# A recurrent layer rearranged: x blocks first, y blocks last, float32 gates, gelu in one function, warm-up matmuls

## The chip, the cores and the metric

The kernel runs on one core of one Trainium2 chip. The metric is the device time of one execution in microseconds (us). Three runs of the kernel before took 1265.87, 1268.60 and 1271.18 us, so their median is 1268.6.

## What is computed

The program is a decoder of two layers over 512 positions of width 1024, all in float32. The first layer is recurrent, the second is attention, and each is followed by a SwiGLU feed-forward. The change is in the recurrent layer:

```python
def recurrent_mixer(h, w_in, conv_w, conv_b, ga_w, ga_b, gx_w, gx_b, lam, w_out):
    proj = h @ w_in                                    # h: rms-normed, 512 x 1024; proj: 512 x 2048
    y_branch, x_branch = jnp.split(proj, 2, axis=-1)
    gate = jax.nn.gelu(y_branch, approximate=True)
    xc = causal_depthwise_conv(x_branch, conv_w, conv_b)          # 4 taps
    hr = rg_lru(xc, ga_w, ga_b, gx_w, gx_b, lam)
    return (gate * hr) @ w_out

# rg_lru, with block-diagonal gates of 8 blocks of 128 x 128:
    r_gate = sigmoid(einsum(xb, w_a) + b_a);  i_gate = sigmoid(einsum(xb, w_x) + b_x)
    log_a = -8 * r_gate * softplus(-lam);     a = exp(log_a)
    u = sqrt(-expm1(2 * log_a)) * (i_gate * x)
    h[t] = a[t] * h[t-1] + u[t]
```

## The kernel before, in words

Activations lie transposed: eight tiles of 128 channels x 512 positions. A float32 value is held as two float32r halves, high and low, and a product is three float32r matmuls (`mm3`: high by high, low by high, high by low, lines 134 to 136). A weight block of 128 output channels (128 x 1024 elements, 512 KB) comes by `Stream`: it is loaded into a ring of two buffers `wr` on SP's DMA queue (line 78), ScalarE casts the high half (line 92), and the low half is made either by a subtract on VectorE (line 99) or, for eight of the sixteen input blocks, by a negating pass on ScalarE (line 95) and a DMA of GpSimd that adds the weights from memory (line 96). Three pairs of halves are held at a time. These casts and subtracts are given a high priority.

A scheduler takes the instructions in program order, with the priorities, and lays down at compile time the order in which every engine issues them; each engine then runs its list in that order and waits where an operand isn't there yet. There are eight PSUM banks: four tagged "mm" for the block products, two "PT", one "S" and one "O".

The recurrent layer (lines 259 to 427) runs so. x comes as eight tiles, and each is scaled by the norm's gain and split (line 205 on ScalarE, 206 on VectorE). The first two input blocks run side by side over k as the tiles come. Then the squares of x are summed (`squares`), the third block runs, and after it come the norm's factors: column sums by TensorE (line 226), some ten small VectorE steps (`rsqrt`), a product of a float32 128 x 512 tile with ones (line 239) and a copy by ScalarE to `rb` (line 241). No result of an input block leaves its PSUM bank before `rb` is there, since `x_block` and `y_block` multiply by it first (lines 332 and 395).

The sixteen input blocks follow `lru_order`: x blocks are numbers 8 to 15, y blocks 0 to 7, and from the sixth on x and y blocks take turns. `x_block` writes the scaled rows, does the convolution (ScalarE one tap, VectorE three) and splits the result. Two blocks later `x_gates` does the two gate products, each by `mm3`, then two sigmoids, a tanh and a product. After each four x blocks `recur` does the decay by exp, a Square, the square root, and the scan in time on VectorE (line 386). `act_order` keeps runs of one activation function together on ScalarE, since a change of function set costs an `ACT_TABLE_LOAD`. `y_block` does the gelu in four steps around a Square and a tanh; `y_gate` multiplies by the scanned state and splits. The gate weights are loaded through the same ring `wr`, on ScalarE's DMA queue, and split (`load_gates`). The output product then takes eight blocks one after the other, each over all eight gated blocks in the order of k.

## Time and profile before

| | |
|---|---|
| time of the profiled execution | 1268.64 us |
| its span | 1266.9 us |
| TensorE matmul, busy | 1218.9 us (96%), 5634 instructions |
| VectorE, busy | 705.9 us (56%) |
| ScalarE, busy | 521.2 us (41%) |
| GpSimd, busy | 192.6 us (15%) |
| mean granted clock of TensorE | 0.984 |

The span runs from the first instruction to the last; a clock of 1.00 is the full level of 2.4 GHz, 0.5 the low one of 1.2 GHz. A TensorE instruction's recorded length overlaps that of the next, so the distance between two starts is its cost. In the rows, PE is TensorE, DVE VectorE, ACT ScalarE, SP the DMA queue of that name, and L134 is line 134.

### The profile page before, as it was taken

The numbers are of one execution on the slowest core, as the hardware profiler recorded it, in microseconds if no ns is written. First come the engines' busy times: TensorE is split into PE (matmuls) and PEld (weight loads), VectorE is DVE, ScalarE is ACT, GpSimd is POOL, SyncE is SP. The second block draws the span as 40 slices with busy tenths as digits, with TensorE's granted clock in tenths as the row PEclk, the third lists the DMA queues.
The fourth block names the chain that finished last, engine by engine and source line by source line (L and its number), as shares of the span: only waits on it lengthen the run. The fifth ranks groups of instructions, "written<-read, shape, count | busy, mean of one in ns | idle before, by whom it ended". The sixth has DMA issues, their size and how long they took to land.

```text
span 1266.9 us, 14906 instructions
## 1 busy us (share of the span) xinstructions
PE 1218.9 (96%) x5634; PEld 1010.3 (80%) x5634; DVE 705.9 (56%) x1292; ACT 521.2 (41%) x964; POOL 192.6 (15%) x172
## 2 busy tenths in 40 slices
PE   7899899999999999999998899899999999999998
PEld 6678688888888888887876777888888888888887
DVE  7788855554455333396566665785754455552221
ACT  5798532332322222266534554554432322332210
POOL 0100001111011000011333355422111011110000
PEclk9899999999999999999999999799999999999999
DMA  5454232223332333332422121001323332223431
GB/s 200 123 135 114 78 100 87 96 100 100 100 100 92 95 93 107 105 102 84 132 68 82 52 67 51 17 18 51 99 85 101 100 100 96 89 94 100 122 119 46
DMA packets 36649, 117.19 MB, mean 93 GB/s; under 512 B 4449, under 2 KB 6625, under 8 KB 36577
## 3 DMA queue, kind: packets, MB, share of 16 engines
q1 hardware_dynamic: 34416, 110.17, 27.6%
q0 software_dynamic: 1152, 4.19, 1.8%
q10 hardware_dynamic: 1008, 1.88, 0.5%
q8 instruction: 44, 0.72, 0.2%
q14 instruction: 29, 0.23, 0.1%
HBM read 113.08 MB, written 2.10 MB: 91 GB/s over the span
## 4 chain that ended last, share of the span: by engine, by line
PE 78%; DVE 12%; ACT 7%; issue 1%; DMA 1%; SPq 0%; DVEq 0%; ACTq 0%
PE ps L135 22%; PE ps L134 22%; PE ps L136 22%; DVE kn L600 3%; PE ps L641 3%; PE ps L643 3%; PE ps L642 3%; ACT junk L583 1%; ACT wh L92 1%; PE ps L716 1%; PE ps L786 1%; DVE kn L610 1%; DVE wl L99 1%; DVE pr L771 1%; DVE gated L386 1%
## 5 line engine op out<-in xcount | busy, mean ns | idle before, releaser
L92 ACT CAST wh<-wr 128x1024 fp32r<-128x1024 f32 (+2 forms) x206 | 210.9, 1024 | 506.8 <-PE ps L135 443.2
L134 PE MATMUL ps<-xh,wh 128*128 128x512 f32 x896 | 353.5, 395 | 12.1 <-ACT xh L205 6.0
L136 PE MATMUL ps<-xh,wl 128*128 128x512 f32 x896 | 351.1, 392 | 0.0
L135 PE MATMUL ps<-xl,wh 128*128 128x512 f32 x896 | 350.8, 391 | 0.0
L99 DVE TENSOR_TENSOR wl<-wr,wh 128x1024 fp32r<-128x1024 f32 (+2 forms) x166 | 240.0, 1447 | 151.9 <-ACT wh L92 151.8
L134 PEld LDWEIGHTS ps<-xh,wh 128*128 128x128 f32 x896 | 169.4, 189 | 48.2 <-DVE xp L332 6.3
L136 PEld LDWEIGHTS ps<-xh,wl 128*128 128x128 f32 x896 | 169.3, 189 | 35.6 <-issue 0.2
L135 PEld LDWEIGHTS ps<-xl,wh 128*128 128x128 f32 x896 | 169.5, 189 | 35.3 <-issue 0.5
L136 PE MATMUL ps<-gh,wl 128*128 128x512 f32 x352 | 137.1, 389 | 0.0
L134 PE MATMUL ps<-gh,wh 128*128 128x512 f32 x352 | 137.1, 389 | 0.0
L135 PE MATMUL ps<-gl,wh 128*128 128x512 f32 x352 | 137.1, 389 | 0.0
L451 POOL TENSOR_TENSOR u<-u,g 128x512 f32<-128x512 f32 x44 | 58.7, 1334 | 507.3 <-ACT wh L92 363.8
L450 DVE TENSOR_TENSOR u<-ps,rb 128x512 f32<-128x512 f32 x44 | 30.4, 691 | 139.2 <-PE ps L136 139.2
L99 POOL TENSOR_TENSOR wl<-wr,wh 128x1024 fp32r<-128x1024 f32 x32 | 77.1, 2409 | 193.2 <-ACT wh L92 141.8
L641 PE MATMUL ps<-wh,xh 128*128 128x512 f32 x224 | 93.2, 416 | 0.0
L643 PE MATMUL ps<-wh,xl 128*128 128x512 f32 x224 | 89.4, 399 | 0.0
L642 PE MATMUL ps<-wl,xh 128*128 128x512 f32 x224 | 89.1, 398 | 0.0
L134 PEld LDWEIGHTS ps<-gh,wh 128*128 128x128 f32 x352 | 66.1, 188 | 13.8
L136 PEld LDWEIGHTS ps<-gh,wl 128*128 128x128 f32 x352 | 66.1, 188 | 13.6
L135 PEld LDWEIGHTS ps<-gl,wh 128*128 128x128 f32 x352 | 66.1, 188 | 13.6
L448 DVE TENSOR_TENSOR g<-ps,rb 128x512 f32<-128x512 f32 x44 | 30.4, 691 | 63.9 <-PE ps L136 63.8
L209 ACT CAST gh<-u 128x512 fp32r<-128x512 f32 x44 | 27.4, 622 | 60.8 <-POOL u L451 60.8
(213 smaller groups left out, 1558.7 us busy)
## 6 DMA issues: line engine op xcount, KB each, us to landing
wr<-in_f_in SPq DMA_DIRECT2D x88, 512.0 KB, 3.5
wr<-in_f_out SPq DMA_DIRECT2D x32, 512.0 KB, 3.5
wr<-in_w_q SPq DMA_DIRECT2D x24, 512.0 KB, 3.5
wr<-in_w_in SPq DMA_DIRECT2D x14, 512.0 KB, 4.1
wr<-in_f_out SPq DMA_DIRECT2D x16, 384.0 KB, 3.1
wr<-in_w_kv SPq DMA_DIRECT2D x12, 512.0 KB, 3.5
wl<-in_w_in POOLq DMA_DIRECT2D x8, 512.0 KB, 7.2
wr<-in_a_out SPq DMA_DIRECT2D x8, 512.0 KB, 3.7
```

The costliest lines, as they stand in the source:

```text
L92: nc.scalar.copy(hi[:, c], r[:, c])
L99: eng.tensor_tensor(lo[:, c], r[:, c], hi[:, c].bitcast(F32), ALU.subtract)
L134: PE.matmul(ps, wh, xh, start=first, stop=False)
L135: PE.matmul(ps, wh, xl, start=False, stop=False)
L136: PE.matmul(ps, wl, xh, start=False, stop=last)
L448: V.tensor_tensor(g, pair[0], rb, ALU.mult)
L450: V.tensor_tensor(u, pair[1], rb, ALU.mult)
L451: G.tensor_tensor(u, u, g, ALU.mult)
L600: V.scalar_tensor_tensor(dst[:, c], dst[:, c], r[:, nh * t + i:nh * t + i + 1], grow[:, g_row, :], ALU.mult, ALU.mult)
L641: PE.matmul(ps[t], xh[k][:, r], wh[:, c], start=k == 0, stop=False)
L642: PE.matmul(ps[t], xh[k][:, r], wl[:, c], start=False, stop=False)
L643: PE.matmul(ps[t], xl[k][:, r], wh[:, c], start=False, stop=k == 7)
```

## The change

The diff does these things. A float32 product of ones runs ten times ahead of everything else on TensorE. The parameters and the first weight block are loaded on ScalarE's DMA queue instead of SP's. The splits of x are held in their order and given a high priority, as are the squares, and the next VectorE subtract of a weight block is put behind the last sum of squares. The norm's column sums stand in the middle of the third block and its row factors in the middle of the fourth; the factors are copied by VectorE; a fifth block uses a bank tagged "PT" before the factors are needed. All x blocks come before all y blocks. The gate weights stay float32, in buffers of their own on SP's queue, and each gate product is one float32 product in place of three float32r matmuls. The root of the decay is taken from a tanh of half the argument and multiplied by 1 + a, with no Square. The gelu is one activation function, after the last square root. The y blocks are gated when both halves of the recurrence are done. The first two output blocks run side by side over k.

The diff, cut to its core:

```diff
@@ -47,6 +47,12 @@
     return a, b, v - a - b
 
 
+def behind(tc, inst, f):
+
+    tc.add_manual_dep(inst.ins, f.ins.name, mybir.DependencyInfo(
+        mybir.DependencyClass.NoSync, mybir.DependencyReason.DATA), reason="order")
+
+
 class Pool:
 
 
...
+
+    def _load(self, i, queue=None):
         ap = self.pieces[i][0]
         r = self.pool.tile([128, 1024], F32, name=f"wr{i}", tag="wr", bufs=2)
         w = ap.shape[-1]
         self.raw[i] = (r, w)
-        return [lambda c=c: self.nc.sync.dma_start(r[:, c], ap[:, c]) for c in self._cuts(i, w)]
+        return [lambda c=c: (queue or self.nc.sync).dma_start(r[:, c], ap[:, c]) for c in self._cuts(i, w)]
 
     def _cuts(self, i, w):
         return [slice(0, 512), slice(512, 1024)] if i < self.halved else [slice(0, w)]
...
+                    a = eng.tensor_tensor(lo[:, c], r[:, c], hi[:, c].bitcast(F32), ALU.subtract)
+                    if self.hold and eng is nc.vector:
+                        behind(self.tc, a, self.hold)
+                        self.hold = None
 
         return [lambda c=c: do(c) for c in self._cuts(i, w)]
...
-    def start(self, n):
...
 
         self.halved = self.nl = self.ns = n
-        loads, splits = zip(*[(self._load(i), self._split(i)) for i in range(n)])
+        loads, splits = zip(*[(self._load(i, None if i else first), self._split(i)) for i in range(n)])
         return [[x[j] for x in y] for y in (loads, splits) for j in range(2)]
 
     def load_to(self, i):
...
 
-    lru_order = [8, 9, 10, 11, 12, 0, 13, 1, 14, 2, 15, 3, 4, 5, 6, 7]
+    lru_order = [8, 9, 10, 11, 12, 13, 14, 15, 0, 1, 2, 3, 4, 5, 6, 7]
     p_in = add_pieces([A["w_in"][m] for m in lru_order[:4]])
...
                 step()
 
-        load_a, load_b, split_a, split_b = ws.start(2)
-        nc.sync.dma_start(par, A["par"])
+        G.memset(ones, 1.0)
+        load_a, load_b, split_a, split_b = ws.start(2, nc.scalar)
+        nc.scalar.dma_start(par, A["par"])
         for k in range(KB):
             nc.sync.dma_start(h[k], A["x"][k])
             run(load_a if k == 0 else load_b if k == 2 else ())
-        G.memset(ones, 1.0)
+        idle = bank("S")
+        for _ in range(10):
+            PE.matmul(idle[:, 0:128], ones, ones, start=True, stop=True)
         G.memset(ident, 0.0)
         G.affine_select(ident, ident, pattern=[[-1, 128]], compare_op=ALU.not_equal, fill=1.0,
                         base=0, channel_multiplier=1)
...
 
         def split(src, gain, hi, lo):
-            S.activation(hi, src, AF.Copy, scale=gain)
+            a = S.activation(hi, src, AF.Copy, scale=gain)
             V.scalar_tensor_tensor(lo, src, gain, hi.bitcast(F32), ALU.mult, ALU.subtract)
+            return a
 
         def halve(src, hi, lo, eng=None):
...
-                V.tensor_add(ssum, ssum, sq)
+                return V.tensor_add(ssum, ssum, sq)
 
         def gain(c, k):
...
 
-        def norm_rows(pool, r, tag="sq", bufs=1):
+        def norm_rows(pool, r, tag="sq", bufs=1, copy=S.copy):
...
             rb = pool.tile([128, T], F32, name="rb", bufs=1)
-            S.copy(rb, ps)
+            copy(rb, ps)
             return rb
 
         def out_proj(p0, nk, per, act_h, act_l, after):
...
             small = Pool(ls)
             for k in range(KB):
-                split(h[k], gain(C_AN, k), xh[k], xl[k])
+                with tc.high_priority():
+                    a = split(h[k], gain(C_AN, k), xh[k], xl[k])
+                    if k:
+                        behind(tc, a, before)
+                    before = a
                 run(split_a if k == 0 else split_b if k == 3 else ())
-            def in_block(i):
-                ps = bank()
+
+            def in_block(i, tag="mm", between=None):
+                ps = bank(tag)
                 wh, wl = ws.get(i)
                 for k in range(KB):
                     c = slice(128 * k, 128 * k + 128)
                     mm3(ps, (wh[:, c], wl[:, c]), (xh[k], xl[k]), k == 0, k == KB - 1)
+                    if k == 3 and between:
+                        between()
                 return ps
 
             parts = [ws.get(0), ws.get(1)]
...
                 for ps, (wh, wl) in zip(first, parts):
                     mm3(ps, (wh[:, c], wl[:, c]), (xh[k], xl[k]), k == 0, k == KB - 1)
-            for k in range(KB):
-                squares(k, lp, "q", 2)
-            first.append(in_block(2))
-            r = norm_factors(small)
-            rb = norm_rows(lp, r, "q", 2)
+            gw = [lp.tile([128, 1024], F32, name=f"gw{i}", bufs=1) for i in range(2)]
+            for g in range(2):
+                nc.sync.dma_start(gw[g], A["gates"][g])
+            with tc.high_priority():
+                for k in range(KB):
+                    ws.hold = squares(k, lp, "q", 4)
+            norm = []
+
+            def soon(fn, *args):
+                with tc.high_priority():
+                    norm.append(fn(*args))
+
+            first.append(in_block(2, between=lambda: soon(norm_factors, small)))
+            first.append(in_block(3, between=lambda: soon(norm_rows, lp, norm[0], "q", 4, V.tensor_copy)))
+            rb = norm[1]
+            first.append(in_block(4, "PT"))
 
 
             lam = par[:, C_LAM:C_LAM + 8]
-            sp8, nsp8 = (small.tile([128, 8], F32, name=n, bufs=1) for n in ("sp8", "nsp8"))
+            sp4, nsp8 = (small.tile([128, 8], F32, name=n, bufs=1) for n in ("sp4", "nsp8"))
             l1 = small.tile([128, 8], F32, name="l1", bufs=1)
             l2 = small.tile([128, 8], F32, name="l2", bufs=1)
...
+            V.tensor_scalar(sp4, sp4, 4.0, None, ALU.mult)
 
             def perm(t):
                 return t.rearrange("q (n i p) -> q n p i", n=4, i=32, p=4)
...
+            hgh = [lp.tile([128, T], F32R, name=f"hgh{k}", bufs=1) for k in range(KB)]
+            hgl = [lp.tile([128, T], F32R, name=f"hgl{k}", bufs=1) for k in range(KB)]
+
+            gated = [lp.tile([128, T], F32, name=f"gated{k}", bufs=1) for k in range(KB)]
+            rate, tau, runs, done = [None] * 4, [None] * 4, [], []
 
             def act_order(inst):
 
-                tc.add_manual_dep(inst.ins, last_act[0].ins.name, mybir.DependencyInfo(
...
             def x_block(b, i):
                 ps = first.pop(0) if first else in_block(i)
-                xp = lp.tile([128, 640], F32, name="xp")[:, :T + 4]
+                xp = lp.tile([128, 640], F32, name="xp", bufs=3)[:, :T + 4]
                 G.memset(xp[:, 0:3], 0.0)
                 V.tensor_tensor(perm(xp[:, 3:3 + T]), mine(ps), mine(rb), ALU.mult)
-                xc = lp.tile([128, T], F32, name="xc", bufs=3)
...
-
-            def x_gates(b, xc, ch, cl):
+                return b, xc
+
...
-                mm3(pr, (gw[0][:, c], gw[1][:, c]), (ch, cl), True, True)
-                mm3(pi, (gw[2][:, c], gw[3][:, c]), (ch, cl), True, True)
+                PE.matmul(pr, gw[0][:, c], xc, start=True, stop=True)
+                PE.matmul(pi, gw[1][:, c], xc, start=True, stop=True)
                 sl = slice(T * (b % 2), T * (b % 2) + T)
                 if b % 2 == 0:
                     rate[b // 2] = lp.tile([128, 2 * T], F32, name="rate", bufs=3)
                     tau[b // 2] = lp.tile([128, 2 * T], F32, name="tau", bufs=3)
                 r = rate[b // 2][:, sl]
-                if b % 4 == 0 and b:
-                    act_order(S.activation(r, pr, AF.Sigmoid, bias=gain(C_GA, b)))
-                else:
-                    S.activation(r, pr, AF.Sigmoid, bias=gain(C_GA, b))
...
             def recur(half):
 
-
+                end_run()
                 for j in range(4):
                     b = 4 * half + j
-                    sl = slice(T * (b % 2), T * (b % 2) + T)
-                    a, t = rate[b // 2][:, sl], tau[b // 2][:, sl]
-                    e = S.activation(a, a, AF.Exp, scale=nsp8[:, b:b + 1])
-                    if j == 0:
-                        act_order(e)
-                    q = lp.tile([128, T], F32, name="q")
...
+                    V.scalar_tensor_tensor(gated[b], a, 1.0, gated[b], ALU.add, ALU.mult)
+                end_run()
                 for j in range(2):
                     t = tau[2 * half + j]
-                    e = S.activation(t, t, AF.Sqrt, scale=0.25)
-                    if j == 0:
-                        act_order(e)
+                    done.append(S.activation(t, t, AF.Sqrt))
+                    act_order(done[-1])
                     for i in range(2):
                         b = 4 * half + 2 * j + i
                         sl = slice(T * i, T * i + T)
                         V.tensor_tensor(gated[b], gated[b], t[:, sl], ALU.mult)
                         V.tensor_tensor_scan(gated[b], rate[b // 2][:, sl], gated[b], 0.0, ALU.mult, ALU.add)
-                last_act[0] = e
-
-            hgh = [lp.tile([128, T], F32R, name=f"hgh{k}", bufs=1) for k in range(KB)]
-            hgl = [lp.tile([128, T], F32R, name=f"hgl{k}", bufs=1) for k in range(KB)]
+                end_run()
 
             def y_block(b, i):
-                ps = first.pop(0) if first else in_block(i)
-                y = lp.tile([128, T], F32, name="y")
+                ps = in_block(i)
+                y = lp.tile([128, T], F32, name="y", bufs=4)
                 V.tensor_tensor(y, ps, rb, ALU.mult)
-                t = lp.tile([128, T], F32, name="t", bufs=3)
-                S.activation(t, y, AF.Square, scale=math.sqrt(0.044715))
-                V.scalar_tensor_tensor(t, t, 1.0, y, ALU.add, ALU.mult)
-                S.activation(t, t, AF.Tanh, scale=math.sqrt(2.0 / math.pi))
-                V.scalar_tensor_tensor(t, t, 1.0, y, ALU.add, ALU.mult)
-                return b, t
-
-            def y_gate(b, t):
-                V.tensor_tensor(mine(t), mine(t), perm(gated[b]), ALU.mult)
-                halve(t, hgh[b], hgl[b])
-
-            load_gates()
+                return b, y
+
+            def y_gate(b, y):
+                g = S.activation(y, y, AF.Gelu_apprx_tanh)
+                act_order(g)
+                V.tensor_tensor(mine(y), mine(y), perm(gated[b]), ALU.mult)
+                halve(y, hgh[b], hgl[b])
+
             xs, ys, halves = [], [], 0
             for i, m in enumerate(lru_order):
                 if m < 8:
...
                         recur(halves)
                         halves += 1
-                while ys and ys[0][0] < 4 * halves:
+                while ys and halves == 2:
                     y_gate(*ys.pop(0))
 
-            def after_a(m):
+            def end_a(m, ps):
+                V.tensor_add(h[m], h[m], ps)
                 split(h[m], gain(C_AF, m), xh[m], xl[m])
-                squares(m, lp, "q", 2)
-
-            out_proj(p_aout, KB, KB, hgh, hgl, after_a)
+                squares(m, lp, "q", 4)
+
+            for ms in ((0, 1), *((m,) for m in range(2, 8))):
+                parts = [ws.get(p_aout + m) for m in ms]
+                first = [bank() for m in ms]
+                for k in range(KB):
+                    c = slice(128 * k, 128 * k + 128)
+                    for ps, (wh, wl) in zip(first, parts):
+                        mm3(ps, (wh[:, c], wl[:, c]), (hgh[k], hgl[k]), k == 0, k == KB - 1)
+                for m, ps in zip(ms, first):
+                    end_a(m, ps)
 
 
```

## Rows read from the trace of the kernel before

**Rows 1.** The page, the chain that ended last, shares of the span by engine

```profile
PE 78%; DVE 12%; ACT 7%; issue 1%; DMA 1%; SPq 0%; DVEq 0%; ACTq 0%
```

**Rows 2.** Windows: stretch, its length, busy us (instructions) of each engine, clock, DMA share, GB/s

```profile
38.60:44.60 6.00, 5.97 (x14) 4.67 (x15) 5.81 (x8) 2.87 (x4) 0.20 (x2) 0.52 1.00 222
82.00:87.20 5.20, 3.46 (x15) 2.53 (x15) 5.20 (x8) 5.17 (x7) 0.95 (x2) 1.00 0.75 159
127.00:146.00 19.00, 15.18 (x55) 10.36 (x54) 15.95 (x22) 10.19 (x15) 0.00 (x0) 0.91 0.06 17
...
5.99:171.10 165.11, 152.94 (x634) 121.58 (x635) 131.80 (x203) 118.98 (x163) 7.65 (x14) 0.97 0.45 128
50.00:140.00 90.00, 85.18 (x363) 68.09 (x361) 75.33 (x101) 75.71 (x103) 5.47 (x9) 0.98 0.42 106
...
60.00:70.00 10.00, 10.00 (x46) 8.29 (x45) 5.29 (x8) 9.96 (x16) 1.20 (x3) 1.00 0.74 166
```

**Rows 3.** Timeline of TensorE, 126 to 146: start, us, instruction, [idle before it]

```profile
125.74 0.39 PE L136 MATMUL ps<-hgh,wl 128*128 128x512 f32 x1
...
127.10 0.39 PE L136 MATMUL ps<-hgh,wl 128*128 128x512 f32 x1
129.91 1.65 PE L134 MATMUL ps<-hgh,wh 128*128 128x512 f32 x3 [2.43 <-ACT hgh L209]
```

**Rows 4.** Timeline of TensorE, 0 to 13

```profile
7.21 0.80 PE L134 MATMUL ps<-xh,wh 128*128 128x512 f32 x1 [0.42 <-ACT wh L92]
...
10.54 0.40 PE L134 MATMUL ps<-xh,wh 128*128 128x512 f32 x1
```

**Rows 5.** Timeline of TensorE, 30.5 to 40

```profile
31.60 1.10 PE L239 MATMUL ps<-dg,ones 128*128 128x512 f32 x2 [0.40 <-DVE dg L238]
32.13 0.79 PE L136 MATMUL ps<-xh,wl 128*128 128x512 f32 x1
38.63 0.80 PE L134 MATMUL ps<-xh,wh 128*128 128x512 f32 x1 [5.71 <-DVE xp L332]
```

**Rows 6.** The chain that ended last, 20 to 50: start, us, what

```profile
30.69 4.24 DMA wr<-in_w_in
...
37.01 0.48 ACT rb L241
```

**Rows 7.** Timeline of ScalarE, 0 to 100: its first weight cast

```profile
4.69 0.62 ACT L92 CAST wh<-wr 128x512 fp32r<-128x512 f32 x1 [1.62 <-DMA wr<-in_w_in]
```

**Rows 8.** Timeline of TensorE, 181.5 to 185: the float32 product in the feed-forward

```profile
182.95 1.02 PE L239 MATMUL ps<-dg,ones 128*128 128x512 f32 x2
...
184.03 0.40 PE L135 MATMUL ps<-xl,wh 128*128 128x512 f32 x1
```

**Rows 9.** Timeline of VectorE, 0 to 100: the first small step of the factors

```profile
25.86 0.16 DVE L228 TENSOR_SCALAR nrv<-ps 128x4 f32<-128x4 f32 x1 [0.88 <-PE ps L226]
```

**Rows 10.** Lines, 0 to 172: instructions by shape, count, busy us, mean ns, idle before

```profile
L99 DVE TENSOR_TENSOR wl<-wr,wh 128x1024 fp32r<-128x1024 f32 x16 | 19.4, 1221 | 2.1 <-ACT wh L92 2.1
...
L404 DVE TENSOR_TENSOR t<-t,gated 128x512 f32<-128x512 f32 x8 | 8.5, 1073 | 0.0
...
L395 DVE TENSOR_TENSOR y<-ps,rb 128x512 f32<-128x512 f32 x8 | 5.5, 688 | 0.8 <-PE ps L136 0.8
...
L370 ACT ACT_TABLE_LOAD x3 | 3.8, 1283 | 0.0
```

**Rows 11.** Timeline of ScalarE, 0 to 100: a table load and what follows it

```profile
45.79 1.28 ACT L356 ACT_TABLE_LOAD   x1
47.09 0.69 ACT L356 ACTIVATE rate<-ps,par 128x512 f32<-128x512 f32 x1
```

**Rows 12.** Timeline of VectorE, 0 to 100: steps back to back

```profile
40.45 3.40 DVE L337 SCALAR_TENSOR_TENSOR xc<-xp,par,xc 128x512 f32<-128x512 f32 x5 [0.18 <-ACT xc L335]
...
72.12 1.29 DVE L385 TENSOR_TENSOR gated<-gated,tau 128x512 f32<-128x512 f32 x2 [0.68 <-ACT tau L379]
...
75.07 2.33 DVE L386 TENSOR_TENSOR_SCAN gated<-rate,gated 128x512 f32<-128x512 f32 x2
```

More of the change, by code (lines that the diff above doesn't have):

```diff
@@ L98, in do, with start @@
                     eng = nc.gpsimd if kind == "pool" else nc.vector
-                    eng.tensor_tensor(lo[:, c], r[:, c], hi[:, c].bitcast(F32), ALU.subtract)
+                    a = eng.tensor_tensor(lo[:, c], r[:, c], hi[:, c].bitcast(F32), ALU.subtract)
+                    if self.hold and eng is nc.vector:
+                        behind(self.tc, a, self.hold)
+                        self.hold = None
         return [lambda c=c: do(c) for c in self._cuts(i, w)]
-    def start(self, n):
+    def start(self, n, first):
         self.halved = self.nl = self.ns = n
-        loads, splits = zip(*[(self._load(i), self._split(i)) for i in range(n)])
+        loads, splits = zip(*[(self._load(i, None if i else first), self._split(i)) for i in range(n)])
         return [[x[j] for x in y] for y in (loads, splits) for j in range(2)]
```

38 lines of the change are left out of this document (15 added, 23 removed).

## The prediction

> **What bounds the kernel now.** I read the page first: TensorE holds 78% of the chain that ended last, VectorE 12% and ScalarE 7% [rows 1]. So time is won only where TensorE waits or its clock is low, and lost where it gets more work. The windows come next: from the first matmul at 5.99 to the end of the recurrent layer at 171.1 TensorE loses time in four stretches [rows 2]. The diff touches this layer alone, and what follows (feed-forward, attention, feed-forward) keeps its code. A matmul of 512 columns starts 0.227 us after the one before it (125.74 to 127.10 is six spacings, [rows 3]); the layer has 384 of them for the input blocks, 48 for the gates, 192 for the output, 624 x 0.227 = 141.5 us, and 1.7 us for the norm. It takes 165.1, so some 22 us are lost, and they can be named:
> - Start: a wait of 1.0 us (5.99 to 7.21, less one matmul), then eight spacings at the low level (7.21 to 10.54 is 3.33 us, at 0.227 it would be 1.8): 1.5. Together 2.5 [rows 2, 4].
> - The norm factors: TensorE starts nothing from 32.13 to 38.63 (6.3 us lost), and comes back at the low level: the stretch 38.6 to 44.6 has a granted clock of 0.52 and 14 matmuls in 6.0 us, which is 2.8 more than at 0.227. Together 9.1 [rows 2, 5]. The chain shows why: the gate weights pass through the two buffers of the weight ring (load, cast and subtract, up to 30.7), only then does the next weight load start, its casts on ScalarE stand ahead of the copy of the factors (L241 at 37.0), and only the factors let VectorE empty the first PSUM bank [rows 6].
> - 82.0 to 87.2: 15 matmuls in 5.2 us, 1.8 lost to casts and subtracts of the gates' halves [rows 2].
> - 127 to 146: 55 matmuls in 19.0 us, 6.5 lost: the output product waits for the last gated blocks, longest at 129.91, and after that gap the low level is back (clock 0.91 over the stretch) [rows 2, 3].
>
> **The change part by part.** The profiled execution took 1268.64 us for a span of 1266.9, and the median of the runs shown is 1268.6, so the sum is made against 1268.6.
>
> Start. The parameters and the first weight block go to ScalarE's DMA queue: three issues ahead of its first work, whose first cast starts at 4.69 [rows 7]; at the length of that cast, 0.62 each, they would still fit. SP's queue begins with x and is three issues shorter. Ten float32 products of 128 columns, once "ones" is filled at 0.9, keep TensorE busy: a float32 product of 512 columns takes 0.85 us (182.95 to 184.03 holds one and one 0.227 matmul, [rows 8]), so a quarter is 0.21 at the full level and 0.43 at the low one, 2 to 4 us in all, over at 3 to 5.3, before data are there at 5.99. If the level is full by 7.2 and the wait for the second weight block goes, 2.5 come back; if not, nothing; and a warm-up that ends late costs at most 0.5. I take 2.2 back, as squares no longer stand between the casts of x.
> The Trainium skill (TensorE: Matmul & The Clock Gate, part 1) says that the number of slow matmuls at a start varies between runs of one kernel; here eight run slow at the start and fourteen after the gap [rows 2, 4]. By that rule alone the 1.5 us of the start would come back in one run and not in another, and the sum would be 1254.7 in the one and 1256.2 in the other; it stands without the rule.
>
> Norm factors. The gate weights stay float32 in buffers of their own: two casts and two subtracts and the detour through the ring go. The squares' sum stands ahead of the third block's subtract, the factors are cut into blocks 2 and 3, the copy goes to VectorE, and block 4 uses a PT bank, so TensorE has five blocks instead of four before it needs an empty bank. Block 2 starts at 10.54 + 39 x 0.227 = 19.4 now, at 17.2 then [rows 4]; half of it later (19.9, or 20.9 with the delay below) come the column sums, which I put at one float32 product, 0.85, then 4.5 us of small VectorE steps (25.86 to 31.60 now, less the gate subtract of 1.22 among them), the product 0.85 and a copy priced as L395, 0.69: factors at about 27.5 instead of 37.5 [rows 5, 6, 8 to 10]. Block 5 wants its bank at 17.2 + 3 x 5.44 + 1.3 = 34.8, and the first bank is free at 28.5. All 9.1 come back. New cost: the low half of block 2's weights is subtracted after seven sums of 0.65 on VectorE. Eight splits at 0.68 and four half subtracts at 0.65 from 5.3 on end at 13.3, the sums at 17.9, the subtract at 19.1, and block 2 wants it at 17.7; some sums can run between the splits, so 1.0 (0 to 2.3) [rows 7, 12].
>
> Gates. 48 matmuls x 0.227 = 10.9 become 16 float32 products: x 0.85 = 13.6, plus 2.7 on TensorE, all on the path [rows 8]. Bounds: a product as cheap as two 0.227 matmuls gives -3.6, the recorded length of 1.02 gives +5.4 [rows 8]. Per block a cast on ScalarE (0.62) and a subtract on VectorE (0.69) go, and with them the waits at 82 to 87: -1.8.
>
> Decay and gelu. The Squares of the decay and of the gelu (16, each as long as a cast, 0.62) and two VectorE steps of each y block (16, each as L395, 0.69) go; tanh goes straight to sqrt without VectorE between [rows 7, 10]. ScalarE had 12 table loads in the layer, three at L370 alone [rows 10], since y blocks' tanh fell between the square roots; with runs of sigmoid, exp, sqrt, twice, then gelu it should be 8. None of this is on TensorE's path by itself; at the change from the first four to the second four x blocks a run of exp, sqrt and sigmoid (three loads, 3.9 us, plus eight passes at 0.62) holds ScalarE for 8.8 us, while the gate bank S allows one block at a time. TensorE can go on with input blocks while banks last; I charge 1.0 (0 to 3).
> The Trainium skill (ScalarE: Activation LUTs, "What ACT_TABLE_LOAD costs") puts a switch at 1.28 us and a drain of 1.38; the trace shows the load at 45.79 and the next activation at 47.09, so no drain [rows 11]. By the page the run would hold ScalarE for 12.9 us and my charge would be its upper end, 3, and the sum 1256.7.
>
> y last and the interleaved output. TensorE would end the y blocks at 34.8 + 8 x 1.7 + 11 x 5.44 = 108.3. Then two output blocks run side by side over k, so the last gated block is wanted only 42 matmuls (9.5 us) later, at 117.8; its chain (multiply, gelu, multiply, cast, subtract: 0.69 + 0.62 + 1.07 + 0.62 + 0.69, [rows 7, 10]) ends 3.7 after the block. So the 6.5 come back, if VectorE keeps up. VectorE's work from the factors on, at back-to-back spacings: an x block 1.07 + 3 x 0.68 + 3 x 0.65 + 1.17 = 6.2, a y block 0.65 + 1.07 + 0.65 = 2.4, seven weight subtracts of 1.22: 8 x 8.6 + 8.5 = 77 us [rows 10, 12]. From 27.5 to 117.8 it has 90: it needs 85% of the time. From 50 to 140 it was busy 75.3 of 90 us, 84% too [rows 2]. That is the edge, so I charge 1.0 (0 to 12, below).
>
> Sum: -2.2 - 9.1 - 1.8 - 6.5 + 2.7 + 1.0 + 1.0 + 1.0 = -13.9, or 1254.7 us.
>
> **The rivals.**
> (1) VectorE lags. At a busy share of 75% the last gated block comes at 27.5 + 77/0.75 = 130, 12 us late: 1265.7 with the 1.0 taken out; at 80%, 6 us late, it is 1259.7. For it: VectorE's share was only 0.53 from 60 to 70, when a table run held ScalarE [rows 2]. Against: x-side work is ready long before, since TensorE is ahead.
> (2) Slower: the same place, but the y blocks' gating can't start before the second recurrence, and no other work fills VectorE while ScalarE does exp, sqrt and gelu of the second half. It decides below a share of 68%: 77/0.68 = 113, the last block at 140.7, 23 us late, 1276.6 and more. For it: y comes last by order and y has four buffers, so little waits ready. Against: no share so low held for longer than 10 us.
> (3) The factors come no earlier: if the sums or block 3's subtract hold up the small steps, 8 of the 9.1 stay: 1262.8. Against: the load that held them is gone from the path.
> (4) The change doesn't do at the start what it says: data of x, not the clock, set the pace up to 10 us, or the warm-up ends too early: 2.2 less, 1256.9.
>
> **How the numbers follow.** Forecast 0.62 (own range 1249 to 1259), rival 1 0.18, rival 4 0.08, rival 3 0.07, rival 2 0.05. A measurement of this kernel tells 0.5%, 6.3 us, from no change. Faster: 0.62 + 0.08 + more than half of rival 1 (0.11) + a little of rival 3 (0.02) = 0.83; slower 0.05; the rest, 0.12, is no change. Range: best is all 22 us back, less 2.7, some 19, and 3 us of spread between runs (1265.87 to 1271.18): 1247; up to rival 1 just above 75%: 1265.
>
> **What would show it.** Right: the first feed-forward matmul at about 157 instead of 171.1; the gap at 32 to 38 gone and the copy of the factors on VectorE before 30; no stretch of clock under 1 between 10 and 155; 16 pairs of gate passes at 0.85; output starting near 108. Wrong: a gap of TensorE ahead of the output with VectorE busy (rival 1) or idle behind ScalarE (rival 2), a gap in block 2 or 3 ahead of the column sums (rival 3), slow spacings past 7.2 (rival 4). It is wrong altogether if the layers behind, whose code is unchanged, take another time.

## The result and the profile after

The changed kernel takes 1258.92 us (median of four runs, 1258.78 to 1260.56) and the kernel before 1267.82 (also four): a ratio of 0.993, 95% interval 0.9906 to 0.9954. It is faster by 8.9 us, 0.7%; 13.9 was forecast. The profiled execution took 1258.78 us for a span of 1257.0, which is 9.9 less than the one of before, and the windows say where that lies. The page of after, the shares of the chain that ended last:

```profile
PE 82%; DVE 11%; ACT 5%; issue 1%; DMA 1%; ACTq 0%
```

Against [rows 1] TensorE has a larger share of a shorter chain: waits went, and hardly any of its work (its matmuls are busy 1218.4 us, 1218.9 before). Windows of after, with the columns of [rows 2]: the layer, the feed-forward behind it, the attention layer up to the last output product, and three stretches inside the recurrent layer:

```profile
6.38:165.11 158.73, 152.36 (x618) 117.94 (x619) 114.70 (x176) 98.33 (x131) 7.50 (x13) 0.99 0.47 131
165.11:525.78 360.67, 360.67 (x1595) 298.47 (x1593) 163.27 (x173) 107.03 (x130) 29.79 (x22) 1.00 0.30 95
525.78:1133.36 607.58, 580.93 (x2881) 486.86 (x2879) 378.32 (x879) 270.58 (x645) 152.45 (x126) 0.98 0.25 80
27.50:117.80 90.30, 85.58 (x339) 63.51 (x338) 70.15 (x93) 66.91 (x86) 7.50 (x13) 0.99 0.51 122
38.60:44.60 6.00, 5.28 (x17) 2.94 (x17) 5.93 (x9) 4.69 (x6) 0.10 (x1) 1.00 0.72 162
116.40:119.80 3.40, 3.40 (x10) 2.62 (x9) 1.99 (x3) 0.62 (x1) 0.00 (x0) 0.50 0.44 154
```

The same two stretches behind the layer in the kernel before:

```profile
171.10:531.78 360.68, 360.68 (x1594) 298.52 (x1593) 163.31 (x173) 106.98 (x130) 29.72 (x22) 1.00 0.31 95
531.78:1142.77 610.99, 585.47 (x2880) 491.20 (x2879) 377.92 (x879) 270.44 (x645) 152.33 (x126) 0.97 0.25 80
```

The feed-forward now starts at 165.11 instead of 171.1: the layer gave 6.0 us. The feed-forward is the same to 0.01. The attention stretch, whose code is unchanged, is 3.4 shorter, at a clock of 0.98 against 0.97; the 0.5 that is left lies in the tail. TensorE in after, 0 to 31:

```profile
0.99 4.64 PE L201 MATMUL ps<-ones 128*128 128x128 f32 x20 [0.99 <-POOL ones L193]
6.38 0.79 PE L145 MATMUL ps<-xh,wh 128*128 128x512 f32 x1 [0.74 <-ACT wh L99]
6.97 0.63 PE L146 MATMUL ps<-xl,wh 128*128 128x512 f32 x1
7.39 0.63 PE L147 MATMUL ps<-xh,wl 128*128 128x512 f32 x1
9.67 1.30 PE L145 MATMUL ps<-xh,wh 128*128 128x512 f32 x2 [1.65 <-ACT xh L219]
...
22.05 0.39 PE L145 MATMUL ps<-xh,wh 128*128 128x512 f32 x1
...
29.57 1.02 PE L254 MATMUL ps<-dg,ones 128*128 128x512 f32 x2
```

The warm-up is there from 0.99 on and ends before the data come. Yet the first matmul starts 0.4 later than before, the spacings are 0.43 (6.97 to 7.39), the low level, there is a wait at 9.67, and the third block (its first matmul is the 49th on x) starts at 22.05; before it was 19.43. (The clock column says 1.00 ahead of the first change on record; in this stretch the spacing tells the level.) ScalarE in after, 5 to 10, shows why x is late:

```profile
5.71 0.62 ACT L99 CAST wh<-wr 128x512 fp32r<-128x512 f32 x1 [0.55 <-DMA wr<-in_w_in]
7.86 0.62 ACT L99 CAST wh<-wr 128x512 fp32r<-128x512 f32 x1 [1.54 <-DMA wr<-in_w_in]
8.38 0.62 ACT L229 ACTIVATE ssum<-h 128x512 f32<-128x512 f32 x1
8.91 0.71 ACT L219 ACTIVATE xh<-h,par 128x512 fp32r<-128x512 f32 x1
```

The second weight cast waits 1.54 us for its load and starts at 7.86 (6.54 before); behind it stand a square of x and then the second cast of x, for which TensorE waits at 9.67. At 29.57 the product of the factors waits for nothing. VectorE in after, their copy:

```profile
30.63 0.69 DVE L256 COPY rb<-ps 128x512 f32<-128x512 f32 x1 [2.61 <-PE ps L254]
```

The gap of [rows 5] is gone, and the low clock of 38.6 to 44.6 with it. TensorE's waits in after, 0 to 172 (line waited for, total us, times, longest):

```profile
PE ps L376 <- DVE xc L370: 2.1, 1, 2.1
PE ps L147 <- DMA wl<-in_w_in: 1.9, 1, 1.9
PE ps L145 <- ACT xh L219: 1.6, 1, 1.6
PE ps L201 <- POOL ones L193: 1.0, 1, 1.0
PE ps L145 <- ACT wh L99: 0.7, 1, 0.7
PE ps L377 <- DVE xp L365: 0.7, 1, 0.7
```

The first is the gate product at 76.36. VectorE in after, 62 to 78, shows it behind the first half's recurrence:

```profile
64.66 1.29 DVE L406 TENSOR_TENSOR gated<-gated,tau 128x512 f32<-128x512 f32 x2 [1.68 <-ACT tau L401]
65.87 2.33 DVE L407 TENSOR_TENSOR_SCAN gated<-rate,gated 128x512 f32<-128x512 f32 x2
68.12 1.26 DVE L406 TENSOR_TENSOR gated<-gated,tau 128x512 f32<-128x512 f32 x2
69.31 2.33 DVE L407 TENSOR_TENSOR_SCAN gated<-rate,gated 128x512 f32<-128x512 f32 x2
71.55 1.20 DVE L106 TENSOR_TENSOR wl<-wr,wh 128x1024 fp32r<-128x1024 f32 x1
72.67 0.74 DVE L370 SCALAR_TENSOR_TENSOR xc<-xp,par,xc 128x512 f32<-128x512 f32 x1
```

The second is at 114.86. The chain of after, 95 to 122:

```profile
101.35 2.96 DVE y L419 x3
...
104.33 0.02 ACT hgh L224
...
104.86 1.05 ACT wh L99
105.91 0.97 ACT wl L102
...
107.16 7.66 DMA wl<-in_w_in
...
114.86 0.50 PE ps L147
```

The casts of the gated blocks wait on ScalarE for VectorE's product; the cast of a weight block stands behind them; then GpSimd's adding DMA takes 7.66 us. TensorE stands 1.9 us for the weights of an input block and comes back at the full level; 1.5 us later the clock falls to the low one (0.50 from 116.40 to 119.80). The output product itself starts at 121.59 and runs to 165.11 with no wait: 192 matmuls in 43.52, exactly 0.227 each.

### The profile page after: what moved, and what is told of

Same layout as the page of the kernel before. It is cut to its first block, busy times and chain, and to the rows that moved or that the text cites. A ratio compares the mean times of both kernels' runs of the same rounds, so it can differ in the third digit from the quotient of the medians.

```text
span 1257.0 us, 14865 instructions
## 1 busy us (share of the span) xinstructions
PE 1218.4 (97%) x5638; PEld 1006.5 (80%) x5638; DVE 689.4 (55%) x1267; ACT 500.8 (40%) x933; POOL 192.6 (15%) x172
## 4 chain that ended last, share of the span: by engine, by line
PE 82%; DVE 11%; ACT 5%; issue 1%; DMA 1%; ACTq 0%
PE ps L145 23%; PE ps L146 23%; PE ps L147 23%; DVE kn L623 3%; PE ps L664 3%; PE ps L666 3%; PE ps L665 3%; ACT junk L606 1%; PE ps L809 1%; DVE kn L633 1%; PE ps L739 1%; DVE pr L794 1%; DVE gated L407 1%; ACT wh L99 1%; DMA wl<-in_w_in 1%
```

## The experiments

Each experiment gives its edit against the changed kernel, or against the kernel before where that is said, then what was expected and what came. The time is that of one run where no ratio stands beside it, and a median of four where one does. "Third block" is the start of the 49th matmul on x (19.43 before, 22.05 after), "feed-forward" the end of the layer (171.1 and 165.11).

**1. One queue again.**

```diff
-        load_a, load_b, split_a, split_b = ws.start(2, nc.scalar)
-        nc.scalar.dma_start(par, A["par"])
+        load_a, load_b, split_a, split_b = ws.start(2, nc.sync)
+        nc.sync.dma_start(par, A["par"])
```

> The changed kernel, with the parameters and the first weight block loaded on SP's queue again, as before; the warm-up matmuls and the order of the splits stay. In the changed kernel the third input block starts at 22.05 us, against 19.43 before, the second block's first weight half is cast at 7.86 against 6.54, and the clock is low until 14.0 against 10.2. Theory: two queues share the transfer rate, so what is wanted first lands later; with one queue that cast comes back to 6.5 to 6.9 and the third block starts at 19.5 or earlier, so some 2.5 us of the whole come back. Rival: the held order and priority of the splits are what is late; then the third block stays at 21.5 to 22.5.

Measured: 1257.41 us; third block 18.71, feed-forward 163.76. TensorE, 0 to 19, has these rows among others:

```profile
7.81 0.39 PE L147 MATMUL ps<-xh,wl 128*128 128x512 f32 x1
8.04 0.39 PE L146 MATMUL ps<-xl,wh 128*128 128x512 f32 x1
...
18.71 0.39 PE L145 MATMUL ps<-xh,wh 128*128 128x512 f32 x1
```

The second queue cost the start 3.3 us; the rival, that the order of the splits is late, is out. On one queue the parameters land 1.8 us after their issue, on two 3.4. 2.0 of the 3.3 are given back later: the same waits for `xc` and for the adding DMA follow, at 73 and 113.5, and now a low stretch comes behind each.

**2. No warm-up.**

```diff
-        idle = bank("S")
-        for _ in range(10):
+        for _ in range(0):
```

> The changed kernel without the ten warm-up matmuls. Theory: they end at 5.6 us, a gap follows, and the clock isn't up when the first real matmuls come, so they bring nothing: the clock rises at the same time (about 14 us) and the third input block starts within 0.4 us of 22.05. Rival 1: they do bring the clock up earlier; without them it stays low some 3 us longer and the third block starts 1.5 us later, 23.5. Rival 2: they stand in the way; without them the first matmul starts before 6.38 and the third block before 21.5.

Measured: 1260.46 us; third block 22.61, feed-forward 165.14, 0.03 later than with it. The third block is 0.56 later, more than the 0.4 of the theory and far from the rival's 1.5. With the data late the warm-up gives this layer nothing that one profile can show.

**3. The last two input blocks split by VectorE, without the adding DMA.**

```diff
-    add_pieces([A["w_in"][m] for m in lru_order[4:]], "dma", 3)
+    add_pieces([A["w_in"][m] for m in lru_order[4:14]], "dma", 3)
+    add_pieces([A["w_in"][m] for m in lru_order[14:]])
```

> The changed kernel, with the low halves of the last two input blocks (y blocks 6 and 7) made by a subtract on VectorE instead of a ScalarE pass and an adding DMA. In the changed kernel TensorE waits 2.0 us at 112.6 to 114.9 for such a DMA, and runs at the low clock from 116.4 to 119.8, 1.6 us more. Theory: the adding DMA (7 us from its issue) is the last link there, so both go and the first feed-forward matmul comes at 161 to 162 instead of 165.1. Rival: VectorE is the bound in that stretch, and two more subtracts of 1.2 us on it make the gated blocks late: the wait moves to the first output matmuls and the feed-forward starts at 164 or later.

Measured: 1257.31 us; feed-forward 163.88. The wait at 114.9 and its low stretch are gone, and from the sixth block to the output it takes 76.1 us instead of 78.2, though the gap at 77 has a low stretch in this profile, which it had not in the other. So the DMA was the last link; the feed-forward came some 2 us later than expected, 0.8 of it from the third block (22.82).

**4. The kernel before with the gate weights out of the ring**, loaded on ScalarE's queue as there, into two spare tiles.

```diff
-                    r = wp.tile([128, 1024], F32, name="gr", tag="wr", bufs=2)
+                    r = lp.tile([128, 1024], F32, name="gr", tag="rate", bufs=3)
```

> The kernel before with one thing changed: the raw gate weights are loaded into two tiles of their own (those of the rate, idle then) instead of the weight ring; same queue, still cast and subtracted. Theory: the detour through the ring is what held the norm factors; without it the weight loads and casts come 8 us earlier, the copy of the factors moves from 37.0 to about 30, and the wait of 6.3 us at 32 to 38.6 shrinks to under 1.5, with its low clock after it; whole time 5 to 9 us less. Rival: the copy stands behind the weight casts in ScalarE's order whatever is loaded where, and the four banks are full at 32; then the copy stays past 33 and at least 3 us of the wait remain.

Measured: 1260.66 us; feed-forward 165.33. The gap at 32 to 38 shrinks to 0.7, but the gate loads, free to start at 0.73, share the transfers with the first data: TensorE's first matmul comes at 9.23 instead of 5.99. Again a second queue delays what is wanted first: the parameters, first on SP's queue as before, land after 3.7 us. From the third block (21.70) to the sixth it takes 21.1 us, where the kernel before takes 30.2: the 9.1 of the gap.

**5. The first recurrence two blocks later.**

```diff
-                    if st[0] % 4 == 3:
+                    if st[0] in (5, 7):
```

> The changed kernel, with the first recurrence (blocks 0 to 3) placed after the gates of block 5 instead of after those of block 3. In the changed kernel TensorE waits 2.3 us at 76.4 for the gates of block 6, whose convolution stands behind the four scans on VectorE. Theory: that place in VectorE's order is the cause, so the wait there falls under 0.5 us and the first feed-forward matmul comes at 162.5 to 163.5 instead of 165.1 (not earlier, if the wait for the adding DMA at 114.9 stays). Rival: VectorE is short of time as a whole, so the wait only moves to the second recurrence or to the gating of y, and the feed-forward starts at 164.5 or later.

Measured: 1253.87 us; feed-forward 158.28, 6.8 sooner than in after and 4 to 5 sooner than expected. Its waits of TensorE, 0 to 172:

```profile
PE ps L145 <- ACT xh L219: 1.5, 1, 1.5
PE ps L201 <- POOL ones L193: 1.0, 1, 1.0
PE ps L377 <- DVE xp L365: 0.7, 1, 0.7
PE ps L145 <- ACT wh L99: 0.3, 1, 0.3
PE ps L376 <- ACT rate L383: 0.3, 1, 0.3
```

Both waits went, the one for `xc` and the one for the adding DMA, and with them the low stretch. The third block came at 20.93, 1.1 sooner, where the edit does nothing; the other 5.7 are 2.1 and 1.9 for the two waits and 1.7 for eight matmuls that ran at the low level. How the DMA wait went, ScalarE shows, 97 to 101:

```profile
98.48 1.03 ACT L99 CAST wh<-wr 128x1024 fp32r<-128x1024 f32 x1
...
100.77 0.63 ACT L224 CAST hgh<-y 128x512 fp32r<-128x512 f32 x1 [0.29 <-DVE y L419]
```

Here the last weight cast ahead of an adding DMA stands before the casts of the gated blocks; in after it stands behind three of them (104.33, then 104.86). ScalarE's order is laid down at compile time, and the edit changed it too. VectorE's product ahead of the first of these casts comes at 99.66 instead of 101.27, and 1.1 of that is the start. In the four profiles that have the wait (after and experiments 1, 2 and 9) the weight cast stands behind three casts of gated blocks; where it stands ahead of them (experiments 5, 6, 7, 11 and 12) there is no wait. So the two waits went with one edit but by two ways, and experiment 3 had taken away the last link of the second.

**6. Split gates again**, three float32r matmuls for each gate product, with the weights in buffers of their own as in experiment 4 and the halves of `xc` in the tiles of the gated blocks; three buffers for the squares instead of four.

```diff
-                PE.matmul(pr, gw[0][:, c], xc, start=True, stop=True)
-                PE.matmul(pi, gw[1][:, c], xc, start=True, stop=True)
+                mm3(pr, (gw[0][:, c], gw[1][:, c]), (ch, cl), True, True)
+                mm3(pi, (gw[2][:, c], gw[3][:, c]), (ch, cl), True, True)
```

> The changed kernel, with the gates as three float32r products of halves again (weights loaded into tiles of their own and split, the convolution's result split by a cast and a subtract). One more difference: three buffers for the squares instead of four. Theory of the sum: 16 float32 products at 0.85 us cost TensorE 2.7 us more than 48 at 0.227, so the gates' matmuls take 10.9 instead of 13.6; but the eight casts and subtracts come back on ScalarE and VectorE, and waits of about 1.8 us at the gates with them: first feed-forward matmul at 163.5 to 164.5 instead of 165.1. Rival: VectorE has no room, 8 x 0.69 us more on it make the wait at 76 and the one ahead of the output longer: 166 or later.

Measured: 1253.72 us; feed-forward 158.25, 6.9 sooner, and 5 to 6 sooner than expected. 2.8 of that is TensorE's own work (48 x 0.227 against 16 x 0.853). In the rest the wait near 76 is down from 2.1 to 1.3 (at 78.46), and the one at 114.9 is gone with its low stretch: the weight cast stands ahead of the gated blocks' casts here too (98.63, then 101.74), though the recurrence is where it was. What float32 gates saved on ScalarE and VectorE (104.1 and 121.6 us of the layer here, 98.3 and 114.7 in after) was time that TensorE didn't wait for.

**7. The old block order** (x and y in turns), six buffers for `y`, everything else changed.

```diff
-    lru_order = [8, 9, 10, 11, 12, 13, 14, 15, 0, 1, 2, 3, 4, 5, 6, 7]
+    lru_order = [8, 9, 10, 11, 12, 0, 13, 1, 14, 2, 15, 3, 4, 5, 6, 7]
```

> The changed kernel with the input blocks in the order of before (x and y in turns from the sixth on) and six buffers for y instead of four; y is still gated when both recurrences are done. Theory: x first is what frees the end of the layer. In the old order the last x block is the eleventh, not the eighth, the second recurrence ends three blocks later (16 us: 117 instead of 101), all y blocks are gated after it, and the output waits 4 us or more: feed-forward at 168 or later, 3 us or more lost. Rival: the order only moves the waits; the one at 76 goes, one of the same size comes at the end, and the feed-forward starts within 1.5 us of 165.1.

Measured: 1263.56 us; feed-forward 169.84. As expected, waits for the gated halves (2.5 and 1.2) stand at the start of the output, with a low stretch behind; the wait near 76 stays (2.0). The new order is worth 4.7 us here.

**8. Experiment 4 with the loads on SP**, behind the fourth weight block.

```diff
-                    r = wp.tile([128, 1024], F32, name="gr", tag="wr", bufs=2)
-                    S.dma_start(r, A["gates"][g])
+                    r = lp.tile([128, 1024], F32, name="gr", tag="rate", bufs=3)
+                    nc.sync.dma_start(r, A["gates"][g])
```

> The kernel before with the raw gate weights loaded into two tiles of their own, on SP's queue behind the fourth weight block. In the run with ScalarE's queue the gate loads went out at 0.7 us and made the first matmul come at 9.2 instead of 6.0, yet from the third input block to the sixth 9.1 us were gained. Theory: the two effects are separate; with the loads behind, the third block starts at 19.4 as before, the sixth at 40 to 41 instead of 49.6, and the feed-forward at 162 to 164 instead of 171.1, so this one edit gives as much as or more than the whole change: 1257 to 1261 us. Rival: the gate loads now delay the weight blocks behind them on the same queue, 4 us or more of the wait come back: 1263 or more.

Measured: 1262.03 us against 1267.29, ratio 0.9958 (0.9942 to 0.9975). Its layer in the windows:

```profile
5.90:165.02 159.12, 152.87 (x635) 120.91 (x635) 130.87 (x203) 118.85 (x163) 7.65 (x14) 0.98 0.48 133
```

This one edit to the kernel before ends the layer at 165.02; the whole change ends it at 165.11. They get there by different ways: from the output's first matmul to the feed-forward it takes 49.9 us here, 50.6 before and 43.5 in after, while after loses 1.9 at the start (third block 20.16 here) and 4.2 from the sixth block to the output (78.2 against 74.0). Time and feed-forward come 1 us later than expected. In the median this edit gives 5.3 us, the change 8.9, and 10.8 in experiment 9; the profile here is of the fastest of four runs. So in time the whole change gives more, and the layer of one profile does not show where.

**9. The changed kernel again**, nothing edited.

> The changed kernel itself, once more, for comparison with the two below on the same chip, and for what differs between two executions of one program. Theory: the feed-forwards and the attention, whose code is unchanged, took 727.0 us from the first feed-forward's end in the profile of this kernel and 730.4 in that of the kernel before, by stretches of low clock in attention alone, which fall anew in every execution; so this figure comes out anywhere from 726.5 to 730.5, the third input block starts at 21 to 23, and the feed-forward at 164 to 167. Rival: the 3.4 us belong to the program; then 727.0 within 0.3. Time 1257 to 1261.

Measured: 1257.03 us against 1267.82, ratio 0.9919 (0.9905 to 0.9934). Windows of its profile, a low stretch at the start, another at 76, and attention:

```profile
7.90:14.70 6.80, 5.92 (x14) 4.54 (x15) 6.60 (x13) 6.80 (x12) 0.00 (x0) 0.50 0.96 355
76.10:79.50 3.40, 3.24 (x5) 1.51 (x5) 3.29 (x6) 2.93 (x4) 0.86 (x1) 0.51 0.09 12
...
524.89:1134.05 609.16, 583.62 (x2880) 489.13 (x2879) 378.37 (x879) 270.51 (x645) 152.42 (x126) 0.98 0.25 80
```

The same program: here the warm-up did raise the level before the first matmul (0.33 from the first start to the second, too short for the low level), it fell again at 7.9, when x was awaited, and the third block came at 21.92, no sooner. The low stretch at 76 was absent in the first profile. The feed-forward starts at 164.22, 0.9 from 165.11, and attention takes 609.16 against 607.58, so the rival is out. Differences of 1 to 2 us between single profiles can't be put down to an edit.

**10. Experiments 1, 3 and 5 together.**

> The changed kernel with three of the edits together: loads of the start on one queue, low halves of the last two input blocks on VectorE, first recurrence after block 5's gates; gates stay float32. Theory: they take away different waits (start 2.2 to 3.3, 76 us 2.3, 115 us 3.8 with its low clock, of which the late recurrence alone took the last two), so the feed-forward starts at 154.5 to 156.5 and the time is 1247 to 1251. Rival: VectorE is full, and the two subtracts make the gated blocks late: 158 or later, 1252 or more.

Measured: 1252.42 us, ratio 0.9879 (0.9865 to 0.9894); third block 19.66, feed-forward 156.98. The feed-forward misses what was expected by 0.5 us and the time by 1.4. The time is that of the rival, but not by its way: no wait for a gated block stands ahead of the output or in it. The feed-forward is at the 157 that the prediction had for the change.

**11. Experiments 1, 5 and 6 together.**

> The changed kernel with loads of the start on one queue, the first recurrence after block 5's gates, and the gates as three products of halves (squares in three buffers). Theory: TensorE saves 2.7 us against float32 gates, and a wait of at most 1.5 us at the gates comes with the casts: feed-forward at 152 to 155.5, time 1244.5 to 1249.5, the fastest of all. Rival: with the recurrence late and the casts back VectorE lags at the gates of blocks 6 and 7, wait of 3 us or more: 156 or later, slower than the float32 version beside it.

Measured: 1248.02 us (1246.78 to 1249.81), ratio 0.9849 (0.9833 to 0.9866): 19.8 us faster than before and, on the same chip, 9.0 faster than the changed kernel (experiment 9). No other kernel here is as fast, as expected. Its layer:

```profile
5.86:153.07 147.21, 146.08 (x635) 117.48 (x635) 120.91 (x184) 103.86 (x140) 7.53 (x13) 1.00 0.51 144
```

and all of TensorE's waits in it, 0 to 172:

```profile
PE ps L201 <- POOL ones L193: 1.0, 1, 1.0
PE ps L145 <- ACT xh L219: 0.7, 1, 0.7
PE ps L145 <- ACT wh L99: 0.6, 1, 0.6
```

The layer takes 147.2 us for 143.2 of matmuls (624 at 0.227, and 1.7 for the norm), at a full clock from first to last. ScalarE and VectorE do more than in the changed kernel (103.9 and 120.9 against 98.3 and 114.7), and TensorE waits less.

**12. Experiment 11 without the warm-up.**

> The fastest version so far (one queue at the start, late first recurrence, gates as products of halves) without the ten warm-up matmuls. In its profile the clock was up from 4.6 us on and never fell in the layer; the third input block started at 18.76, the feed-forward at 153.07, median 1248.0. Theory: with the data in time the warm-ups are worth what the low level costs at the start: without them the clock comes up at 10 to 12 us, the third block starts at 19.4 to 20.2, and the whole is 0.7 to 1.5 us longer, 1248.5 to 1250. Rival: they are worth nothing here either; third block at 18.5 to 19.0, time within 0.5 of 1248.

Measured: 1252.14 us (1251.02 to 1253.84), ratio 0.9868 (0.9851 to 0.9884): 16.6 us faster than the kernel before on its chip, where experiment 11 was 19.8 faster on its own; the two intervals overlap. The time is 2 us above the range that was expected. Its layer:

```profile
5.78:154.26 148.48, 147.44 (x634) 119.90 (x635) 121.08 (x184) 104.23 (x140) 7.50 (x13) 1.00 0.52 143
```

With the data on time the layer ends 1.2 us later without the warm-up, and the third block 1.3 later (20.07 against 18.76), as expected. Attention takes 611.75 against 607.13, 4.6 more and 500 us after the edit; experiment 9 says how little one profile of it tells.

## Why the prediction was right and where it was wrong

Direction and rough size held, and the range (1247 to 1265). By the layer alone the time would be 1268.6 - 6.0 = 1262.6, outside the forecast's own range of 1249 to 1259. That the measured time lies inside it is luck: 3.9 of the 9.9 us between the profiles come from behind the layer, which the prediction put at nothing. One sign of being right failed as well: between 10 and 155 the clock is low twice, up to 14.0 and from 116.4 on. The terms, predicted and measured between the two profiles (the start from the third block, the factors, gates and waits from what TensorE lost there, the output from what is left):

| term | predicted | measured |
|---|---|---|
| start, to the third block | -2.2 | +2.6 |
| norm factors | -9.1 | -8.3 |
| low half behind the sums | +1.0 | 0 |
| gates in float32 | +2.7 | +2.8 |
| waits at 82 to 87, run of tables at the half | -0.8 | +0.2 |
| output | -5.5 | -3.3 |
| the layer | -13.9 | -6.0 |
| attention and tail | 0 | -3.9 |

**The step that failed is the start.** It said "if the level is full by 7.2 and the wait for the second weight block goes, 2.5 come back; if not, nothing". The loss was bounded at 0.5, for a warm-up that ends late, because a transfer that is issued sooner was taken to land no later. Issued beside SP's x, the parameters and the first weights shared the transfers with it and landed later: the first weight cast ran at 5.71 instead of 4.69 [rows 7], the second at 7.86 instead of 6.54. Nor had the squares left the casts of x: one stands ahead of the second, at 8.38. Experiment 1 shows it (-3.3), experiment 4 shows the same with other loads (9.23), and of the other thirteen profiles the seven that start on two queues have the third block at 20.9 to 22.8, the six on one queue at 18.7 to 20.2. The Trainium skill (DMA: Bandwidth & Descriptors, "Queues, rings and completion order") says that each DMA engine serves in turn the queues that have work for it; the landing times of the parameters, 1.8 to 1.9 us on one queue and 3.1 to 3.4 in the seven profiles on two, agree. Rival 4 had the mechanism in its words (data of x set the pace) and its sign came, slow spacings past 7.2; its price was wrong, 2.2 where it was 4.8.

**The factors** went as worked out: copy on VectorE, before 31 rather than 30, no gap. Experiments 4 and 8 show that it was the detour through the ring that made the gap; the cuts and priorities of the change were not needed for it. The subtract behind the sums was charged 1.0 and cost nothing: the third block's runs at 15.50, ahead of the first sum (16.64), and the one behind the sums, at 22.43, is that of the fourth block, which starts at 28.44.

**The gates** hold their row [rows 8]: a product takes 0.86 (40.23 to 41.09), 16 of them 13.7. But the waits that they were to remove go without them: experiment 6 keeps the split gates, in buffers of their own, and waits less.

**Middle and output** were one thing, priced as three. VectorE was not the bound by its share: from 27.5 to 117.8 it was busy 70.15 of 90.30 us, 78%, between the 85% needed and the 75% of rival 1, and the last gated block did not come late. What failed was order, in two places. The recurrence of the first half takes VectorE for eight steps in a row, and the gates' `xc` waits behind it: 2.1 us. And on ScalarE a weight cast stands behind three casts of gated blocks, which wait for VectorE's products behind the second recurrence (95.66 to 104.31 in the chain); the adding DMA passes that on to TensorE: 1.9, and 1.7 for the low stretch. Experiment 5, which moves only the first recurrence, removes both, the second by ScalarE's order that came out with it. That is rival 1's engine in another place and for 5.7 us instead of 6 to 12.

The output itself runs without a wait, as said, and gave 7.1 us (50.6 from its first matmul to the feed-forward before, 43.5 after), more than the 6.5 counted; the wait and the low stretch ahead of it take 3.6 of that back, which leaves about the -3.3 of the table. It starts at 121.59 and not "near 108": 4.9 of the difference is the start, 0.6 lies in the three blocks around the factors, 6.4 are three waits from 42 us on and the low stretch, and some 1.4 stay unexplained.

**ScalarE** has eight loads of a table in the layer, as counted. In after the one ahead of the first square roots runs from 62.27 for 1.28 us, and the next pass starts at 63.57, 0.02 after its end. The drain of 1.38 that the Trainium skill (ScalarE: Activation LUTs, "What ACT_TABLE_LOAD costs") adds is not there, as in [rows 11].

**What lies behind the layer.** The prediction said it would be wrong altogether if the unchanged layers took another time, and attention took 3.4 less. The granted clock shows how. At the same place in the program, 474 us behind the layer's end, it is low in the profile of before and full in that of after:

```profile
645.10:648.50 3.40, 3.40 (x10) 2.87 (x11) 0.00 (x0) 0.59 (x1) 0.00 (x0) 0.50 0.23 94
...
639.10:642.50 3.40, 3.37 (x17) 2.89 (x18) 0.00 (x0) 0.59 (x1) 0.00 (x0) 1.00 0.27 111
```

Before has five such stretches behind the layer, 30.7 us in all, after three with 20.5. From the layer's end to the end of the kernel it takes 1095.8 and 1091.9 us; the changed kernel's second profile (four stretches) takes 1093.5. Over the eleven profiles with the diff it is 1091.7 to 1096.5 (the most in experiment 12), over the three without it 1093.6 to 1095.8. So two executions of one program differ by 1.6 of the 3.9, kernels that share the diff by more than all of it, and nothing ties the 3.9 to the diff. That the change gives more in the medians than experiment 8 (8.9 and 10.8 against 5.3), whose layer ends at the same time, stays open: no run here shows by what way.

## What to carry to other kernels

Ahead of the first matmul the order of landing matters, and not the number of queues: issue what is wanted first alone, and price a second queue as a possible loss. Where a wait ends on a DMA or a cast, follow the chain back to the engine whose order holds it up, and after an edit look at the order of the other engines too; moving one recurrence two blocks later gave 5.7 us, 3.6 of them by a cast that changed its place on ScalarE, while the float32 gates, which cut the work of VectorE and ScalarE, cost TensorE more than they gave. And before a rearrangement, try its smallest part: in one profile two buffers for the gate weights end the layer where the whole change ends it, since parts of the change (the output, 7.1) paid for others (the start, the two waits).

## What the runs showed of the hardware

A warm-up ended at the low level in one execution (spacings of 0.43 at 6.97) and at the full one in another of the same program (0.33 at 6.07), as in the seven profiles of other kernels with it (0.33 to 0.39 between the first two matmuls); so the low level of the first profile was the exception. In six of these eight the level fell again between 7.4 and 9.5, when TensorE waited for x or weights; the two where it did not (experiments 1 and 11) start on one queue, but so does experiment 10, where it did. The rule of the Trainium skill that the prediction weighed (TensorE: Matmul & The Clock Gate, part 1), that the number of slow matmuls at a start varies between runs, agrees: they end at 14.0 in one execution of the changed kernel and run from 7.9 to 14.7 in the other. The third block differed by 0.13 only. A gap of 2.1 at 76.36 had no low stretch behind it in one profile and 3.4 us of it in the other. Two queues whose transfers run at once from the start let the parameters (52 KB) land after 3.4 us instead of 1.9, though more bytes moved in the first 6 us (208 GB/s against 164). An adding DMA of 512 KB had a median of 7.4 us from issue to landing in after, a plain load of the same weights on SP's queue 4.0.
